# An encoder layer on one Trainium2 core: small vectors loaded into the tile of ones, adaLN's products in four column groups

## The chip, the cores and the metric

The kernel runs on one core of a Trainium2 chip. A core has five engines with queues of their own: PE (TensorE, matrix products; PEld is its loading of weights), DVE (VectorE), ACT (ScalarE), POOL (GpSimd) and SP (SyncE, which here only issues DMAs). Products land in PSUM, everything else on chip lies in SBUF, tiles of 128 partitions. The metric is the device time of one execution in microseconds.

## The reference

One layer (D = 1024, 4 heads of 256) over two sequences with shared weights, a prompt of 1024 tokens and a sample of 256, each with one conditioning vector c. What matters here is the modulation at the head of the layer:

```
mod = c @ w_ada + b_ada                       # (1, 1024) @ (1024, 3072), all fp32
shift, scale, gate = split(mod, 3)
h = rms_norm(x, norm_g) * (1 + scale) + shift
p = h @ w_in                                  # 1024 -> 11280 columns
... short convolution, two-way chunkwise mLSTM, gates ...
out = x + gate * (merged @ w_out);  then rms_norm(out, final_norm_g)
```

Nothing of `p` can be computed before `shift` and `scale` are there, and they take 2048 columns of w_ada, 8 MB, for two vectors.

## The kernel before

**Order of work.** The operations of a stage are recorded first, each with its engine, an estimated cost, what it reads and writes, and a step (a priority). A planner, `Board`, plays them through in a model of its own: per engine a time at which it is free, per DMA an issue cost, a common lane of `KB_US` kilobytes a microsecond and a landing delay. It takes the operation that can start first, or one of a lower step within 0.25 us of it on the same engine, and sends them out in that order; each engine then works through its queue strictly in order. `FIRST` is the time at which SP and the lane are taken to begin. The first stage, up to about 1200 us of the execution, is one such plan, made with `KB_US` 385 and `FIRST` 5.0 (L1283). Buffers of a pool (`misc` for PSUM, `raw`, `wh`, `wl`, `comb`, `acc`) are handed out in the order in which the program names them. So a `misc` buffer named later cannot be taken before adaLN has taken its own, whatever the priorities.

**Setting up (L229 to L270).** POOL writes the identity `ident`, two masks and `ones`, a constant tile of 128 x 128 that later products use for sums over partitions and for spreading a row. A tile `rows` from a pool of its own, on the right side of SBUF, takes the small vectors as rows of 128 (c of both sequences, 2 x 1024 of b_ada, norm_g and others): seven DMAs issued by ACT (L244 to L250). PE turns 80 rows into columns (L253), DVE copies them to `cols` (L254), and the pool of `rows` is closed (L255). Every later tile on the right side may lie where `rows` lay.

**The beginning (L390 to L570).** SP loads w_ada in eight loads `w` 0 to 7 of two 512 KB pieces (a piece is 128 of the 1024 input channels by 512 columns of shift and 512 of scale), the ten blocks of x and the first input weights, in the order `w0, x 0-2, w1, w2, x 3-4, w3, raw (0,8)` and then `raw (0,0), w4 to w7, x 5-7, x 8-9, raw (0,4)`, as far as the tiles are free. Loads 0 to 3 make the first half of the channels of shift and scale (`hf` 0), loads 4 to 7 the second. w_ada and x lie in tiles that later hold the multiplied halves of x: b00, b10, b11 (w_ada; b11H takes w4 and then w7), t2, t3, b11L (x). `early_load` brings weights for the *corners*, twelve small products that are done ahead of the rest.

Of each piece adaLN makes two products (L487). The stationary operand is c, for each piece 128 x 4 with two columns in use (`cz4`, in the spare end of a `big` tile, zeroed by POOL at L465 and filled by DVE at L466); the moving one is 128 x 512 of w_ada. All eight products of one kind sum into `t[0:4, j]`, j = 0 for shift and 1 for scale. After the fourth load of a half the two sums (four partitions each) are copied to SBUF, shift by DVE and scale by ACT (L496), turned by eight small PE transposes into a `misc` buffer (L500), and DVE's `modulation` (L474 to L476) makes s1 and shf of them.

`norm_x` scales the blocks of x on DVE and ACT; `turn_x` transposes them on PE (L449), and ACT (L454) or DVE (L457) applies s1 and shf on the way out of PSUM to `xt`. `both_parts` splits the result into a high and a low part (L381 ACT, L382 DVE), `combine` forms sums and differences (L387 DVE) for a Strassen scheme of seven products. The products with w_in are at L770, all stages' weights being split by ACT (L329) and POOL (L330) out of `raw` tiles, with sums of them by DVE (L642); DVE adds their results (L686).

Of the kernel before, what the change touches and what calls it, by code (L numbers as in the profile page):

```python
# [16 lines left out]
P = 128  # L17
D = 1024
# [22 lines left out]
class Board:  # L41
# [25 lines left out]
    def buf(self, pool, shape, dt, tag, bufs, t=None):  # L67
        b = self.Buf(pool, shape, dt, tag, bufs, t)
        self.places.setdefault((id(pool), tag), []).append(b)
        return b  # L70

    def op(self, eng, us, f, r=(), w=(), after=(), low=False, slack=0.0):

        o = self.Op()
        o.eng, o.us, o.f, o.low, o.step, o.n, o.played, o.slack = eng, us, f, low, self.step, len(self.ops), False, slack
        o.before = set(after)
        for t in r:
            if t in self.writer:
                o.before.add(self.writer[t])
        for t in w:  # L80
            o.before.update(self.readers.get(t, ()))
            if t in self.writer:
                o.before.add(self.writer[t])
        for t in w:
            self.writer[t], self.readers[t] = o, []
        for t in r:
            if t not in w:
                self.readers.setdefault(t, []).append(o)
        o.before.discard(o)
        o.bufs = list(dict.fromkeys(b for t in (*r, *w) for b in (t if isinstance(t, tuple) else (t,)) if isinstance(b, self.Buf)))  # L90
        for b in o.bufs:
            b.users.append(o)
        self.ops.append(o)
        return o
# [87 lines left out]
def encoder_kernel(  # L182
# [50 lines left out]
    G.affine_select(out=masks[:, 1, :], in_=masks[:, 1, :], pattern=[[1, P]], compare_op=ALU.is_ge,  # L233
                    fill=NEG, base=0, channel_multiplier=-1)
    ones = const.tile([P, P], F32, name="ones")
    G.memset(ones[:], 1.0)
    zero = const.tile([P, 1], F32, name="zero")
    V.memset(zero[:], 0.0)


    RC, RNG, RMH, RCW, RCB, RSH, NR = 0, 16, 24, 32, 56, 64, 80
    r0stack = ctx.enter_context(ExitStack())
    rows = r0stack.enter_context(tc.tile_pool(name="rows", bufs=1, side="right")).tile([P, P], F32, name="rows")
    A.dma_start(rows[0:8, :], c_prompt.rearrange("a (r p) -> (a r) p", p=P))  # L244
    A.dma_start(rows[8:16, :], c_sample.rearrange("a (r p) -> (a r) p", p=P))
    A.dma_start(rows[RSH:RSH + 16, :], b_ada[0, 0:2 * D].rearrange("(r p) -> r p", p=P))
# [5 lines left out]
    pt = psA.tile([P, 512], F32, tag="misc", name="misc")  # L252
    PE.transpose(pt[:, :NR], rows[:NR, :], ident[:NR, :NR])  # L253
    V.tensor_copy(cols[:, :NR], pt[:, :NR])  # L254
    r0stack.close()  # L255
    mhq = const.tile([P, KT], F32, name="mhq")
    V.tensor_scalar(out=mhq[:], in0=cols[:, RMH:RMH + 8], scalar1=0.25, scalar2=None, op0=ALU.mult)

# [131 lines left out]
    def beginning():  # L390
        junks = [((lambda b=b: b[:, 0:D]), b) for b in (big(), big())]

        def cz4():
            return junks[0][1][:, D:D + 32].rearrange("p (k s) -> p k s", s=4)

        def load_wa(i):

# [65 lines left out]
        cv_ = cols[:, 0:16].rearrange("p (s k) -> p k s", s=2)  # L463
        ctok = ("c",)
        op("POOL", .15, lambda: G.memset(cz4(), 0.0), w=[junks[0][1], ctok])  # L465
        op("DVE", .15, lambda: V.tensor_copy(cz4()[:, :, 0:2], cv_), r=[ctok], w=[ctok])  # L466
        pada = {}

        def modulation(hf, pm):

            ks = slice(4 * hf, 4 * hf + 4)
            pmc = pm[:, 0:32].rearrange("p (h k l s) -> p h k l s", h=2, l=2, s=2)[:, :, :, 0]
            wide = (lambda c: cols[:, c + 4 * hf:c + 4 * hf + 4].unsqueeze(2).to_broadcast([P, 4, 2]))
            V.tensor_tensor(out=s1[:, ks], in0=pmc[:, 1], in1=wide(RSH + 8), op=ALU.add)  # L474
            V.scalar_tensor_tensor(out=s1[:, ks], in0=s1[:, ks], scalar=1.0, in1=wide(RNG), op0=ALU.add, op1=ALU.mult)
            V.tensor_tensor(out=shf[:, ks], in0=pmc[:, 0], in1=wide(RSH), op=ALU.add)  # L476

        def adaln(i):

            hf = i // 4  # L480
            if i == 0:
                pada.update((n, buf(psX, [P, 2, 512], F32, "acc", 3)) for n in range(2))
            t = pada[hf]
            for n, (wa, tok) in enumerate(wa_at[i]):
                kt = 2 * (i % 4) + n
                for j in range(2):
                    op("PE", .88, lambda j=j, kt=kt, wa=wa: PE.matmul(  # L487
                        t[0:4, j, :], cz4()[:, kt, :], wa()[:, j * 512:(j + 1) * 512],
                        start=kt == 0, stop=kt == KT - 1), r=[ctok, tok], w=[(t, j)])
            if i % 4 < 3:  # L490
                return
            pm = misc_buf()
            for j in range(2):
                m, f = buf(cp, [P, 4, P], F32, "comb", 5), (V.tensor_copy, A.copy)[j]
                row = (lambda m=m: m[0:4].rearrange("p a b -> p (a b)"))
                op(("DVE", "ACT")[j], .6, lambda j=j, f=f, row=row: f(row(), t[0:4, j, :]), r=[(t, j)], w=[m])  # L496

                def turn_mod(j=j, row=row):
                    for r in range(4):
                        PE.transpose(pm[:, 16 * j + 4 * r:16 * j + 4 * r + 4], row()[:, r * P:(r + 1) * P], ident[0:4, 0:4])  # L500

                op("PE", .25, turn_mod, r=[m], w=[(pm, j)])
            op("DVE", .6, lambda: modulation(hf, pm), r=[(pm, 0), (pm, 1)], w=[("s1", hf)])

        def fetch(*items):

# [72 lines left out]
    def misc_buf():  # L579
        return buf(psA, [P, 512], F32, "misc", 2)  # L580
# [698 lines left out]
    for ws in ws_c:  # L1279
        for w in ws:  # L1280
            for b in w:
                b.open = True
    board.KB_US, board.FIRST = 385.0, 5.0  # L1283
    board.play()
    board.KB_US, board.FIRST = Board.KB_US, Board.FIRST
    rstack.close()
# [593 lines left out]
```

## Time and profile before

| | us |
|---|---|
| median of 3 runs | 1692.64 (1692.21 to 1693.99) |
| the profiled execution | 1692.12 |
| its span, first to last instruction | 1690.3 |
| PE busy in it | 1648.8 (98%) |
| DVE / ACT / POOL busy | 989.9 / 575.0 / 677.2 |

A profile page shows one execution: busy times, the span in slices, DMA queues, the chain of waits that ended last, and the costliest groups of instructions. The trace behind it answers narrower questions: who waited for whom, the busy time and the granted clock of TensorE in any stretch, the instructions in order of time. A row of the timeline is start, length, engine, line, operation, the tile written and the tile read, a count, and in brackets how long the engine had been idle and what ended that. `SPq` and `ACTq` are the queues that issue DMAs. A matmul in full fp32 appears as two instructions, one for each pass.

### The profile page before, as it was taken

Reading aid. Unit: us, or ns where it says so; the run is one execution under the profiler, and the core shown is the slowest. Engines: PE = TensorE matmul, PEld = TensorE weight load, DVE = VectorE, ACT = ScalarE, POOL = GpSimd, SP = SyncE. Lnnn points to the kernel's source line nnn. Section 1 sums busy time; section 2 is a strip of 40 time slices with the busy share of each in tenths; the row PEclk is TensorE's granted clock in tenths of the full one; section 3 lists DMA queues with packets and bytes.
Section 4 is the critical chain, followed back from the end, with each engine's and each line's share of the span. In section 5 each row is a group of like instructions: output and inputs, shape, how many; then the busy total and the mean of one; then the engine's idle time right before and its main releaser. Section 6 shows DMA issues by size and latency. Waiting matters only on the chain.

```text
span 1690.3 us, 27664 instructions
## 1 busy us (share of the span) xinstructions
PE 1648.8 (98%) x10526; PEld 1562.4 (92%) x10526; DVE 989.9 (59%) x1688; ACT 575.0 (34%) x1117; POOL 677.2 (40%) x499
## 2 busy tenths in 40 slices
PE   7999999999999999999999999999999999999997
PEld 2699999999999999999999999999988899898985
DVE  4694434556556565566656886662257677555645
ACT  3552332124444222222222212111256665333322
POOL 1133333335565566667666543333210101323412
PEclk9999999999999999999999999999999999999999
DMA  9334325324554222222222556458878855773631
GB/s 318 109 125 139 117 88 125 76 71 128 152 144 111 59 69 69 82 70 67 59 74 74 136 138 145 121 128 269 268 241 293 275 170 177 245 249 105 244 103 63
DMA packets 281527, 240.81 MB, mean 142 GB/s; under 512 B 96068, under 2 KB 236596, under 8 KB 281396
## 3 DMA queue, kind: packets, MB, share of 16 engines
q1 hardware_dynamic: 281216, 239.01, 46.5%
q8 instruction: 83, 1.36, 0.3%
q14 instruction: 48, 0.39, 0.1%
q10 hardware_dynamic: 180, 0.04, 0.0%
HBM read 170.12 MB, written 68.89 MB: 141 GB/s over the span
## 4 chain that ended last, share of the span: by engine, by line
PE 89%; DMA 4%; DVE 4%; SPq 1%; ACT 1%; issue 1%; ACTq 0%; DVEq 0%
PE acc L770 62%; PE u L1399 3%; PE qc L1359 2%; PE accd L1554 2%; PE accd L1555 2%; PE accd L1556 2%; PE accd L1767 2%; PE accd L1768 2%; PE accd L1766 2%; PE acc L1622 2%; PE acc L1621 2%; PE acc L1623 2%; DMA raw<-in_w_in_dram 1%; SPq L318 1%; PE misc L1482 1%; DVE xt L387 1%
## 5 line engine op out<-in xcount | busy, mean ns | idle before, releaser
L330 POOL TENSOR_TENSOR wl<-comb,wh 128x512 fp32r<-128x512 f32 x176 | 246.4, 1400 | 288.0 <-ACT wh L329 268.5
L686 DVE TENSOR_TENSOR q<-acc,q 128x640 f32<-128x640 f32 x272 | 220.8, 819 | 220.3 <-PE acc L770 218.2
L330 POOL TENSOR_TENSOR wl<-raw,wh 128x512 fp32r<-128x512 f32 x136 | 190.6, 1402 | 236.3 <-ACT wh L329 224.4
L770 PE MATMUL acc<-xt,wh 128*128 128x320 f32 x1408 | 265.0, 310 | 2.2 <-DVE xt L382 2.2
L770 PEld LDWEIGHTS acc<-xt,wh 128*128 128x128 f32 x1408 | 220.9, 188 | 3.5 <-DVE xt L382 3.2
L329 ACT CAST wh<-comb 128x512 fp32r<-128x512 f32 x176 | 109.0, 619 | 298.6 <-PE acc L770 288.6
L329 ACT CAST wh<-raw 128x512 fp32r<-128x512 f32 x136 | 84.4, 620 | 269.3 <-PE acc L770 207.3
L770 PE MATMUL acc<-xt,wl 128*128 128x320 f32 x704 | 160.4, 309 | 0.0
L1582 POOL TENSOR_TENSOR wl<-raw,wh 128x512 fp32r<-128x512 f32 x28 | 36.6, 1310 | 224.9 <-ACT wh L1581 175.9
L770 PEld LDWEIGHTS acc<-xt,wl 128*128 128x128 f32 x704 | 117.7, 188 | 0.0
L642 DVE TENSOR_TENSOR comb<-raw 128x512 f32<-128x512 f32 x88 | 72.5, 824 | 43.3 <-DMA raw<-in_w_in_dram 18.4
L837 POOL TENSOR_TENSOR big<-big,q 128x640 f32<-128x640 f32 x48 | 78.2, 1630 | 35.6 <-DVE q L686 27.2
L586 ACT ACTIVATE q<-q,zero 128x640 f32<-128x640 f32 x76 | 63.1, 831 | 79.7 <-DVE q L686 75.3
L642 DVE TENSOR_TENSOR comb<-raw,comb 128x512 f32<-128x512 f32 x44 | 46.1, 1047 | 62.6 <-POOL wl L330 62.5
L770 PE MATMUL acc<-b00H,wh 128*128 128x320 f32 x352 | 81.6, 312 | 0.0
L770 PE MATMUL acc<-b10H,wh 128*128 128x320 f32 x352 | 80.2, 308 | 0.8 <-ACT q L700 0.8
L1554 PE MATMUL accd<-y,wh 128*128 128x320 f32 x256 | 80.3, 314 | 0.6 <-DVE og L1532 0.6
L770 PE MATMUL acc<-b11H,wh 128*128 128x320 f32 x352 | 80.7, 310 | 0.0
L770 PE MATMUL acc<-t2H,wh 128*128 128x320 f32 x352 | 80.4, 309 | 0.0
L770 PE MATMUL acc<-t3H,wh 128*128 128x320 f32 x352 | 80.3, 309 | 0.0
L770 PE MATMUL acc<-t3L,wh 128*128 128x320 f32 x352 | 80.2, 309 | 0.0
L770 PE MATMUL acc<-t3H,wl 128*128 128x320 f32 x352 | 80.2, 309 | 0.0
(312 smaller groups left out, 4120.8 us busy)
## 6 DMA issues: line engine op xcount, KB each, us to landing
raw<-in_w_in_dram SPq DMA_DIRECT2D x108, 256.0 KB
raw<-in_w_in_dram SPq DMA_DIRECT2D x40, 512.0 KB
th<-th_dr SPq DMA_DIRECT2D x32, 320.0 KB
th_dr<-q SPq DMA_DIRECT2D x28, 320.0 KB
raw<-in_w_proj_conv_dram SPq DMA_DIRECT2D x16, 512.0 KB
raw<-in_w_proj_mlstm_dram SPq DMA_DIRECT2D x16, 512.0 KB
raw<-in_w_out_dram SPq DMA_DIRECT2D x16, 512.0 KB
k<-kn_dr SPq DMA_DIRECT2D x56, 128.0 KB
```

Source lines behind the costliest of these rows:

```text
L329: op("ACT", .63, lambda: A.copy(wh[:], src()), r=r, w=[wh])
L330: op("POOL", 1.4, lambda: G.tensor_tensor(out=wl[:], in0=src(), in1=fp(wh[:]), op=ALU.subtract), r=[*r, wh], w=[wl])
L586: A.activation(out, in_, AF.Tanh, bias=zero[:, 0:1], scale=0.5)
L642: op("DVE", .9, lambda: V.tensor_tensor(out=t[:], in0=x(), in1=y(), op=o), r=[x.tok, y.tok], w=[t])
L686: op("DVE", .82, lambda: V.tensor_tensor(out=two(dst()), in0=acc[:, :, 0:TQ], in1=two(t()), op=ALU.add), r=[acc, t.tok], w=[dst.tok])
L770: PE.matmul(acc[:, q, 0:TQ], st_[:, k_, :], m_[:, q * TQ:(q + 1) * TQ], start=k_ == 0 and n == 0, stop=k_ == 3 and n == 2)
L837: op("POOL", 1.65, lambda: G.tensor_tensor(out=dst(), in0=dst(), in1=t(), op=ALU.mult), r=[dst.tok, t.tok], w=[dst.tok])
L1359: PE.matmul(pq[:, 0:HD + 2], qTs[i][:, kd, c * P:(c + 1) * P], C[:, kd, :], start=kd == 0, stop=kd == 1)
L1399: PE.matmul(pu[:, db, 0:HD + 2], k[:, db * P:(db + 1) * P], wv[:], start=True, stop=True)
L1554: PE.matmul(accs[q][:, :TQ], wh, yH, start=kt == 0, stop=False)
L1555: PE.matmul(accs[q][:, :TQ], wh, yL, start=False, stop=False)
L1582: op("POOL", 1.36, lambda wh=wh, wl=wl, src=src: G.tensor_tensor(out=wl[:], in0=src(), in1=fp(wh[:]), op=ALU.subtract), r=[raw, wh], w=[wl])
```

## The change

Four things are changed.

`rows` is no longer a tile of its own: the small vectors are loaded into `ones`, and POOL writes the ones there later, behind the zeroing of c. The pool of `rows` and its closing go.

c's stationary operand becomes 128 x 32 (two columns in use). Each product takes one of four groups of 32 columns of the array, `tile_position=(0, g)`, with g = 32 * (2n + j): n the piece of the load, j shift or scale. The sums land in four groups of 32 partitions of one PSUM bank, each over four of the eight pieces. Two products of a piece are one operation of the plan at 1.1 instead of two at 0.88.

After the fourth load one DVE copy takes all 128 partitions. Four products with `sel`, a 128 x 4 choice of columns made from the identity, turn the sums, add the two groups that belong together and drop the empty columns, instead of eight transposes. ACT's copy goes.

`FIRST` is 1.0 instead of 5.0 for this first plan.

```
     ones = const.tile([P, P], F32, name="ones")
-    G.memset(ones[:], 1.0)
...
-    r0stack = ctx.enter_context(ExitStack())
-    rows = r0stack.enter_context(tc.tile_pool(name="rows", bufs=1, side="right")).tile([P, P], F32, name="rows")
+    rows = ones
...
-    r0stack.close()
...
-            return junks[0][1][:, D:D + 32].rearrange("p (k s) -> p k s", s=4)
+            return junks[0][1][:, D:D + 256].rearrange("p (k s) -> p k s", s=32)
...
         op("POOL", .15, lambda: G.memset(cz4(), 0.0), w=[junks[0][1], ctok])
+        op("POOL", .2, lambda: G.memset(ones[:], 1.0), r=[ctok], w=["ones"])
         op("DVE", .15, lambda: V.tensor_copy(cz4()[:, :, 0:2], cv_), r=[ctok], w=[ctok])
         pada = {}
+        sel = const.tile([P, 2, 2], F32, name="sel")
+        half = (lambda i: ident[:, 64 * i:64 * i + 64].rearrange("p (j r) -> p j r", r=32)[:, :, 0:2])
+        op("DVE", .15, lambda: V.tensor_tensor(out=sel[:], in0=half(0), in1=half(1), op=ALU.add), w=["sel"])
...
-            pmc = pm[:, 0:32].rearrange("p (h k l s) -> p h k l s", h=2, l=2, s=2)[:, :, :, 0]
+            pmc = pm[:, 0:16].rearrange("p (k h s) -> p h k s", h=2, s=2)
...
-                for j in range(2):
-                    op("PE", .88, lambda j=j, kt=kt, wa=wa: PE.matmul(
-                        t[0:4, j, :], cz4()[:, kt, :], wa()[:, j * 512:(j + 1) * 512],
-                        start=kt == 0, stop=kt == KT - 1), r=[ctok, tok], w=[(t, j)])
+                def mm(n=n, kt=kt, wa=wa):
+                    for j in range(2):
+                        g = 32 * (2 * n + j)
+                        PE.matmul(t[g:g + 32, 0, :], cz4()[:, kt, :], wa()[:, j * 512:(j + 1) * 512],
+                                  start=i % 4 == 0, stop=i % 4 == 3, tile_position=(0, g))
+                op("PE", 1.1, mm, r=[ctok, tok], w=[t])
...
-            pm = misc_buf()
-            for j in range(2):
-                m, f = buf(cp, [P, 4, P], F32, "comb", 5), (V.tensor_copy, A.copy)[j]
-                row = (lambda m=m: m[0:4].rearrange("p a b -> p (a b)"))
-                op(("DVE", "ACT")[j], .6, lambda j=j, f=f, row=row: f(row(), t[0:4, j, :]), r=[(t, j)], w=[m])
-                def turn_mod(j=j, row=row):
-                    for r in range(4):
-                        PE.transpose(pm[:, 16 * j + 4 * r:16 * j + 4 * r + 4], row()[:, r * P:(r + 1) * P], ident[0:4, 0:4])
-                op("PE", .25, turn_mod, r=[m], w=[(pm, j)])
-            op("DVE", .6, lambda: modulation(hf, pm), r=[(pm, 0), (pm, 1)], w=[("s1", hf)])
+            pm, m = misc_buf(), buf(cp, [P, 4, P], F32, "comb", 5)
+            op("DVE", .65, lambda: V.tensor_copy(m[:].rearrange("p a b -> p (a b)"), t[:, 0, :]), r=[t], w=[m])
+            def turn_mod():
+                for r in range(4):
+                    PE.matmul(pm[:, 4 * r:4 * r + 4], m[:, r, :], sel[:].rearrange("p j s -> p (j s)"), start=True, stop=True)
+            op("PE", .9, turn_mod, r=[m, "sel"], w=[pm])
+            op("DVE", .6, lambda: modulation(hf, pm), r=[pm], w=[("s1", hf)])
...
-    board.KB_US, board.FIRST = 385.0, 5.0
+    board.KB_US, board.FIRST = 385.0, 1.0
```

## The prediction

> **What bounds the kernel now.** I read the page first, then the waits of SP's queue at the start, the chain of work in order of time, and the busy time by stage.
>
> ```profile
> span 1690.3 us, 27664 instructions
> ```
>
> The page's chain that ended last consists mostly of PE work, so what counts is when PE first runs without gaps and how much it then has left. The page hides what lies before that: who holds back the first load. The waits of SP's queue in the first 20 us show it (time in total, times, longest):
>
> ```profile
> SPq L318 <- DMA rows<-in_norm_g_dram: 2.8, 1, 2.8
> SPq L1867 <- PEq L1867: 0.7, 1, 0.7
> SPq L318 <- DMA rows<-in_conv_w_dram: 0.5, 1, 0.5
> SPq L318 <- PE misc L253: 0.5, 1, 0.5
> SPq L318 <- DMA rows<-in_mh_norm_g_dram: 0.3, 1, 0.3
> SPq L318 <- DMA rows<-in_conv_b_dram: 0.2, 1, 0.2
> ```
>
> SP, which issues every large load, is ready at 0.7 us and then waits 2.8 + 0.5 + 0.5 + 0.3 + 0.2 = 4.3 us for the loads and the turning of `rows`. It has no use for `rows`: the pool of `rows` is closed, and the first tile that SP fills, b00H, lies on the same side of the memory and takes its place. The chain in order of time joins that wait to the rest (start, length, what):
>
> ```profile
> 3.05 1.48 DMA rows<-in_conv_b_dram
> 4.66 0.38 PE misc L253
> 5.06 0.43 SPq L318
> ...
> 45.95 6.63 DMA b11H<-in_w_ada_dram
> ...
> 52.63 1.88 PE acc L487 x4
> ...
> 64.62 0.88 PE acc L770 x6
> ```
>
> From 5.06 us the chain runs through loads to the last piece of w_ada, landed at 45.95 + 6.63 = 52.58 us, then through adaLN's last products. Three stretches of all engines, and one of DVE alone (start:end, length, busy with counts, granted clock, DMA share, GB/s), say what each is bound by:
>
> ```profile
> 5.06:52.58 47.52, 37.73 (x112) 10.82 (x112) 22.98 (x58) 16.39 (x30) 5.94 (x4) 0.96 1.00 343
> 55.64:119.94 64.30, 60.64 (x419) 58.89 (x418) 58.51 (x71) 40.98 (x64) 21.95 (x15) 1.00 0.31 99
> 119.94:1200.00 1080.06, 1075.59 (x7300) 1065.42 (x7300) 612.89 (x794) 305.20 (x521) 546.26 (x394) 1.00 0.40 112
> 53.69:119.30 65.61, 58.54 (x72) 1.00 0.31 97
> ```
>
> First DMA: a share of 1.00 for 47.5 us, with PE idle for 9.8 of them. Then, until 119 us, PE (60.64 of 64.30) and DVE (58.54 of 65.61) are both nearly full, and DVE prepares what PE will multiply. Then PE alone, idle for 1080.06 - 1075.59 = 4.5 us in 1080.
>
> **Part 1: `rows` in the tile of ones.** The constant tile is never given back, so b00H has no predecessor, and SP starts at about 0.7 us. Gain on the path: 4.3 us, if the loads that follow keep their places. They stand one behind the other at a full DMA share, so the last lands at 52.58 - 4.3 = 48.3. The small loads of ACT's queue now travel beside the large ones. Their delay isn't shown, since nothing ran beside them. Bound: none, or all that SP issued before the last of them. SP issues a 512 KB load in about 0.43 us (the 5.06 row), so some six by 3.4 us; 3.1 MB at 343 GB/s is 9 us, which would bring `cols` at 13 us. The lower end is nearer, as the two queues are separate; even the upper end costs little, because adaLN's first half waits for its fourth load anyway (the 25.28 row: 21.0 after the shift), and DVE and POOL stand free:
>
> ```profile
> 25.28 0.08 PEld L487 LDWEIGHTS acc<-b10L,big 128*4 128x4 f32 x1 [0.44 <-DMA b10L<-in_w_ada_dram]
> 2.09 0.12 POOL L465 MEMSET big<- 128x32 f32 x1
> 0.87 0.32 POOL L229 MEMSET masks<- 128x256 f32 x1
> 13.28 1.23 DVE L414 CUSTOM_DVE_ANT_0 big<-t3H 128x1024 f32<-128x1024 f32 x1 [7.60 <-DMA t3H<-in_x_prompt_dram]
> 26.87 5.94 POOL L330 TENSOR_TENSOR wl<-raw,wh 128x512 fp32r<-128x512 f32 x4 [24.66 <-ACT wh L329]
> ```
>
> The zeroing of c grows to the 128x256 form (0.12 to 0.32 us). The ones are now written behind the turning of `rows`; POOL waits there, and behind it stands only the splitting at 26.87, after 24.66 idle us. The sum that makes `sel` is one small DVE operation in the 7.60 idle us before 13.28. All this I count as nothing; without that cover it would be 0.2 us each. `ones` itself is read only by the recurrences and what follows them.
>
> **Part 2: the plan's start, FIRST from 5 to 1.** It issues nothing; it moves the planned arrivals 4 us earlier, as the real ones move, and with the lower PE costs may exchange neighbours. One exchange lies on the path:
>
> ```profile
> 36.06 1.02 PE L487 MATMUL acc<-b11H,big 128*4 128x512 f32 x2
> 38.93 1.07 SPq L318 DMA_DIRECT2D b11H<-in_w_ada_dram  x1
> 40.10 5.76 SPq L318 DMA_DIRECT2D raw<-in_w_in_dram  x2
> 45.95 0.89 SPq L318 DMA_DIRECT2D b11H<-in_w_ada_dram  x1
> raw<-in_w_in_dram SPq DMA_DIRECT2D x108, 256.0 KB
> ```
>
> The last w_ada load overwrites the fifth one's tile, whose products end at 37.1; a pair of `raw` loads slipped between its halves. If those products end earlier in the plan, the second half goes ahead of the pair: 2 x 256 KB at 343 GB/s are 1.5 us. Between 0 and 1.5 I take a gain of 0.7, since the plan's readiness of the two is close.
>
> **Part 3: products in four groups of 32 columns.** Each load of w_ada gives eight matmul instructions (four products, two passes each):
>
> ```profile
> 8.88 5.57 PE L487 MATMUL acc<-b00H,big 128*4 128x512 f32 x8 [3.85 <-DMA b00H<-in_w_ada_dram]
> 15.91 3.60 PE L487 MATMUL acc<-b00L,big 128*4 128x512 f32 x8 [1.46 <-DMA b00L<-in_w_ada_dram]
> ```
>
> At full clock eight end 3.60 us after the first starts, 0.43 us apart: 8 x 8 x 0.43 = 27.5 us over the eight loads. Four products wholly side by side would take 2 x 0.43 = 0.9 us a load; none side by side, 3.4. If instructions start in order, a product's second pass must wait for its first on the same columns, and only the next product's first pass can run beside it: five steps of 0.43, 2.15 us a load. I take that: 8 x 1.3 = 10 us of PE time freed (bounds 0 and 20). Nearly all lies in the stretch where PE waits for loads anyway, so only the end of it counts. The Trainium skill ("TensorE: Matmul & The Clock Gate", Part 3) has matmuls in different column strips run at once, some 4 ns apart; by it a load would take 0.9 us. The same skill ("TensorEngine Tiling (Array Packing)", Key Properties) speaks against the change: changing the tiling mode drains the array, which the transposes in between would pay for. No row here shows either.
>
> The end, after the last arrival (the products' 1.88 us stands above):
>
> ```profile
> 53.69 0.68 DVE L496 COPY comb<-acc 4x512 f32<-4x512 f32 x1 [6.25 <-PE acc L487]
> 54.55 0.57 ACT L496 COPY comb<-acc 4x512 f32<-4x512 f32 x1 [7.97 <-PE acc L487]
> 55.74 0.17 DVE L474 TENSOR_TENSOR s<-misc,cols 128x8 f32<-128x8 f32 x1 [1.38 <-PE misc L500]
> L449 PEld LDWEIGHTS misc<-ident,t3H x16: 137/141/145, 27.8 to 68.2; 128*128 128x128 f32 x16
> ```
>
> Before: products, ACT's copy and its turning: 52.63 to 55.74, 3.1 us. After: two products in three steps of 0.43 (1.3; bounds 0.9 and 1.9), one DVE copy of 0.68 (as long for 128 partitions as for 4, since 512 elements lie in each), four products with 128x128 weights. Weights take 0.14 us; one load each would make 0.6, two passes each 1.1; I take 0.9. With three handovers of 0.1, 3.2 us: no change (bounds -0.7 and +0.9).
>
> **What the freed PE time is worth.** Corner products that need only the first half of s1 can move ahead of the last arrival, out of the stretch where turnings and L770 alternate (the 0.88 us row at 64.62). But until 119 us DVE has 65.61 - 58.54 = 7.1 idle us: no faster PE gains more there, and the idle time mostly follows x's own order. I take 0.5 (bounds 0 and 7.1). After 119.94 the shift passes on, because PE has no slack; a new order could take back some of the 4.5 idle us or add as many: 0.
>
> **Sum:** 4.3 + 0.7 + 0 + 0.5 = 5.5 us. The profiled execution took 1692.12 us (1.8 beyond its span), so 1686.6; the median of the runs is 0.5 higher, 1687.1. A measurement of this kernel can tell about 0.2% from no change, 3.4 us.
>
> **Rivals.** *More (0.12):* products wholly side by side free 20 us, corner work fills the gaps before the last arrival, and the alternating stretch shrinks by DVE's slack. 4.3 + 1.5 + some 5 give 1682, with all 7.1 of it 1680. For it: four weight splits are ready by 33 us. Against it: DVE's 58.5 us have to be done after the arrival.
>
> *A cold PE (0.14):* the granted clock by the microsecond shows that PE, nearly idle, falls to half:
>
> ```profile
> 28.00:29.00 1.00, 0.31 (x3) 0.07 (x1) 0.01 (x1) 1.00 (x3) 1.00 (x1) 1.00 1.04 361
> 30.00:31.00 1.00, 0.78 (x1) 0.09 (x2) 0.47 (x2) 0.43 (x1) 1.00 (x2) 0.50 1.08 406
> 33.00:34.00 1.00, 1.00 (x3) 0.06 (x2) 1.00 (x2) 0.63 (x1) 0.00 (x0) 0.82 1.02 406
> ```
>
> Low load from 28 us, 0.50 from 30, full again after some 3.5 us of work. Shorter products leave longer gaps. If PE is cold when the last piece lands, the end costs 1.3 + 0.9 more, and the next 3.5 us of turnings half as much work, 1.7: 3.9 of the 5.5 go, and 1691 results. Against it: corner products lie ready in those gaps. The Trainium skill ("TensorE: Matmul & The Clock Gate", Part 1) says the same: half rate after an idle window of about 3.4 us; the trace agrees with 0.50 at 30 us.
>
> *Slower (0.08):* the groups don't run side by side and, being seen as little work, never bring the clock up. The first load above ran so: 5.57 us, mostly at double spacing. At twice 0.43 a step, a load's eight instructions take 6.9 us, eight loads 55 us from 8.88 - 4.3 = 4.6 us on: to 59.6 us, past the 54.5 (52.63 + 1.88) at which they end now. Of PE's other work there (37.73 - 27.5, 10 us, some of it time lost cold) I put 4 ahead of the end; then PE, not DMA, sets s1 at about 64 instead of 56: +8, 1700. It decides once a load takes more than 47.5 / 8 = 5.9 us. Against it: the second load ran at full clock with the same duty.
>
> *The wait stays (0.08):* some other owner of b00H's place holds SP back; only parts 2 and 3 act: 1691.4.
>
> **How the numbers follow.** The forecast has 0.58, its own range 1684 to 1689. The range 1681 to 1692.5 takes in the cold PE and the wait that stays, and leaves out half of "more" and the slower case with some chance spread past its ends. Faster than 1689.2: 0.58 + 0.12 and a little of the cold case, 0.72. Within 0.2%: the rest of that and most of the wait that stays, 0.18. Slower: 0.08 and the tail of a worse order later, 0.10.
>
> **What would show it.** Right: SP's first load at about 0.7 us with no wait for `rows`; the last w_ada landing near 47.5 us, with or without the `raw` pair ahead of it; eight L487 instructions in about 2.2 us; PE's last waits for DVE ending near 114 us instead of 119.9; some 4.5 idle us of PE from there to 1200. Wrong: a landing after 50 us, a clock of 0.50 at it, or new idle time in the long stretch of more than 3 us.

## The result and the profile after

The changed kernel takes 1686.66 us (median of 6 runs, 1683.48 to 1689.26), the kernel before on the same chip 1692.51 (1691.66 to 1694.70): a ratio of 0.996, 95% interval 0.9948 to 0.9973. The prediction was 1687.1 in a range of 1681 to 1692.5. The profiled execution took 1686.94 us, 5.18 less than the one of before. The head of its page:

```profile
span 1685.1 us, 27656 instructions
```

The waits of SP's queue in the first 20 us (time in total, times, longest):

```profile
SPq L315 <- DMA b00H<-in_w_ada_dram: 3.1, 1, 3.1
SPq L315 <- DMA b00L<-in_w_ada_dram: 2.7, 2, 1.8
SPq L315 <- DMA ones<-in_b_ada_dram: 1.3, 1, 1.3
```

and the timeline of the same queue, its first loads and, further on, the last w_ada load with its neighbours:

```profile
0.74 0.95 SPq L315 DMA_DIRECT2D b00H<-in_w_ada_dram  x2
4.80 1.99 SPq L315 DMA_DIRECT2D t3H<-in_x_prompt_dram  x2
...
37.39 3.12 SPq L315 DMA_DIRECT2D b11H<-in_w_ada_dram  x2
40.61 3.38 SPq L315 DMA_DIRECT2D raw<-in_w_in_dram  x2
```

The wait for the turning of `rows` is gone and the first load starts at 0.74 instead of 5.06 us. But the load behind it starts only at 4.80: a wait of 3.1 us for the first load itself has come in its place. SP now also waits 1.3 us for a small load, that of b_ada, whose tile it doesn't touch. At the far end the two halves of the last w_ada load now stand together (x2) and the raw pair behind them; before, the pair stood between them.

TensorE's side, adaLN's products, its turning, and the first product of the b22 job (all x is split by then; before at 120.07). The products of the last load's first half, before:

```profile
49.62 1.88 PE L487 MATMUL acc<-b11H,big 128*4 128x512 f32 x4 [0.97 <-DMA b11H<-in_w_ada_dram]
```

and after (PEld is the loading of weights):

```profile
8.47 0.20 PEld L491 LDWEIGHTS acc<-b00H,big 128*32 128x32 f32 x8 [0.91 <-DVE big L464]
8.47 1.94 PE L491 MATMUL acc<-b00H,big 128*32 128x512 f32 x8 [0.70 <-DVE big L464]
...
40.21 1.80 PE L491 MATMUL acc<-b10H,big 128*32 128x512 f32 x8
40.95 0.14 PEld L491 LDWEIGHTS acc<-b10H,big 128*32 128x32 f32 x4 [0.60 <-DMA b10H<-in_w_ada_dram]
...
47.21 1.05 PE L491 MATMUL acc<-b11H,big 128*32 128x512 f32 x4
48.62 1.05 PE L491 MATMUL acc<-b11H,big 128*32 128x512 f32 x4 [0.35 <-DMA b11H<-in_w_ada_dram]
...
50.59 0.95 PE L502 MATMUL misc<-sel,comb 128*128 128x4 f32 x8
...
105.38 0.63 PE L772 MATMUL acc<-xt,wh 128*128 128x320 f32 x2 [3.54 <-DVE xt L379]
...
113.77 0.45 PE L772 MATMUL acc<-b11H,wh 128*128 128x320 f32 x2
```

Two products (four instructions) take 1.05 us instead of 1.88, eight instructions 1.80 instead of 3.60. In the 1.80 the second pair of products waits for its piece of w_ada until 40.95, so that row doesn't show how many can run at once. The row at 8.47 does: there both pieces have landed, all eight weights are loaded within 0.20 us, and eight instructions of 1.06 us each end 1.94 us after the first starts. The four products run wholly side by side, at about half the rate of the later rows, as the first instructions of before did (5.57 us for eight, at 8.88). DVE applies the scale (s1) in this row:

```profile
51.57 0.17 DVE L475 TENSOR_TENSOR s<-misc,cols 128x8 f32<-128x8 f32 x1 [1.16 <-PE misc L502]
```

And the stretches (start:end, length, busy PE, PEld, DVE, ACT, POOL with counts, granted clock, DMA share, GB/s): from s1 to the b22 job, from there to 1200, and two short ones behind TensorE's wait of 3.54 us:

```profile
51.57:113.77 62.20, 58.66 (x403) 57.92 (x403) 55.09 (x71) 40.63 (x63) 20.36 (x14) 0.97 0.29 94
113.77:1200.00 1086.23, 1080.07 (x7315) 1069.44 (x7314) 616.65 (x794) 305.31 (x523) 548.21 (x395) 1.00 0.41 113
106.00:108.00 2.00, 2.00 (x10) 2.00 (x9) 2.00 (x4) 0.81 (x2) 0.00 (x0) 0.50 0.00 0
108.00:110.00 2.00, 2.00 (x12) 2.00 (x12) 1.83 (x3) 0.00 (x0) 0.00 (x0) 0.72 0.00 0
```

The same five points in both kernels add up to the whole difference. The products of the last w_ada load start as its halves land, so the first row shows the stream ahead of the raw pair and the second adds the exchange:

| | before | changed | difference |
|---|---|---|---|
| products of the last w_ada load's first half start | 49.62 | 47.21 | -2.41 |
| products of its second half start | 52.63 | 48.62 | -4.01 (-1.60 more) |
| s1 | 55.74 | 51.57 | -4.17 (-0.16 more) |
| b22 job starts | 120.07 | 113.77 | -6.30 (-2.13 more) |
| end of the span | 1690.3 | 1685.1 | -5.2 (+1.1: given back) |

So the early load is worth 2.4 us and not 4.3, the exchange of the raw pair 1.6 and not 0.7, and 2.1 us come out of the stretch behind s1, in which DVE's busy time fell from 58.64 (between the same two points of before) to 55.09. Single profiles settle such terms only roughly: in changed_again below, the same kernel, they are -1.49, -1.65, -0.16 and -1.38, and the rest gains 1.1 more.

### The profile page after: what moved, and what is told of

It is laid out like the page before. It is cut to its first block, busy times and chain, and to the rows that moved or that the text cites. A ratio compares the mean times of both kernels' runs of the same rounds, so it can differ in the third digit from the quotient of the medians.

```text
span 1685.1 us, 27656 instructions
## 1 busy us (share of the span) xinstructions
PE 1639.5 (97%) x10526; PEld 1565.8 (93%) x10526; DVE 993.3 (59%) x1689; ACT 572.8 (34%) x1115; POOL 679.0 (40%) x499
## 3 DMA queue, kind: packets, MB, share of 16 engines
q8 instruction: 83, 1.36, 0.3%
## 4 chain that ended last, share of the span: by engine, by line
PE 66%; DVE 1%; ACT 0%; issue 0%; DMA 0%; POOL 0%; SPq 0%; DVEq 0%; ACTq 0%; POOLq 0%
PE acc L772 38%; PE u L1401 3%; PE qc L1361 3%; PE accd L1556 2%; PE accd L1557 2%; PE accd L1558 2%; PE acc L1623 2%; PE acc L1624 2%; PE acc L1625 2%; PE accd L1770 2%; PE accd L1768 2%; PE accd L1769 2%; PE misc L1484 1%; PE misc L1444 1%; PE misc L1531 1%
## 5 line engine op out<-in xcount | busy, mean ns | idle before, releaser
L1556 PE MATMUL accd<-y,wh 128*128 128x320 f32 x256 | 80.5, 315 | 0.6 <-DVE og L1534 0.6
L1557 PE MATMUL accd<-y,wh 128*128 128x320 f32 x256 | 80.4, 314 | 0.0
L772 PE MATMUL acc<-b00L,wh 128*128 128x320 f32 x352 | 80.2, 309 | 0.1
```

Of the source, the lines that this page charges most:

```text
L772: PE.matmul(acc[:, q, 0:TQ], st_[:, k_, :], m_[:, q * TQ:(q + 1) * TQ], start=k_ == 0 and n == 0, stop=k_ == 3 and n == 2)
L1556: PE.matmul(accs[q][:, :TQ], wh, yH, start=kt == 0, stop=False)
L1557: PE.matmul(accs[q][:, :TQ], wh, yL, start=False, stop=False)
```

## The experiments

The theory: the reordering by the plan, and DVE's time behind s1, carry most of the gain, while a new wait eats much of what the early start should give. Rival: the earlier start and the faster products are the gain by themselves. All ratios are to the kernel before, run on the same chip (its medians were 1692.78, 1693.27 and 1693.05 in the three sets of runs). The first four rows ran together, then changed_again, rows_pool_queue, combine_pool and pool_queue_combine, then the other four. changed_again is the changed kernel once more; s1 and the stretches are of one profile each.

| kernel | median (range, runs) | ratio, 95% interval | s1 | s1 to b22 | DVE busy in it |
|---|---|---|---|---|---|
| rows_alone | 1690.23 (1689.62-1692.13, 11) | 0.9987, 0.9979-0.9996 | 53.83 | 64.30 | 58.87 |
| rows_first | 1690.96 (1687.21-1691.96, 11) | 0.9984, 0.9975-0.9993 | 53.20 | 64.30 | 58.74 |
| rows_first_raw_behind | 1688.95 (1687.33-1690.88, 9) | 0.9977, 0.9968-0.9987 | 51.80 | 64.49 | 58.63 |
| groups_alone | 1687.97 (1686.03-1689.20, 6) | 0.9971, 0.9959-0.9982 | 54.07 | 60.85 | 54.39 |
| changed_again | 1685.25 (1683.06-1686.36, 5) | 0.9953, 0.9939-0.9966 | 52.44 | 62.95 | 55.10 |
| rows_pool_queue | 1686.34 (1683.43-1687.63, 5) | 0.9959, 0.9946-0.9971 | 49.77 | 63.44 | 56.29 |
| combine_pool | 1689.66 (1688.91-1691.83, 11) | 0.9979, 0.9971-0.9988 | 51.20 | 66.30 | 60.74 |
| pool_queue_combine | 1687.32 (1686.00-1689.74, 7) | 0.9970, 0.9960-0.9981 | 49.94 | 66.26 | 60.84 |
| groups_old_plan | 1689.69 (1686.87-1691.83, 11) | 0.9982, 0.9974-0.9991 | 55.11 | 64.08 | 55.91 |
| splits_before_combine | 1686.47 (1686.08-1687.26, 5) | 0.9964, 0.9951-0.9978 | 51.11 | 62.50 | 55.12 |
| kept_warm | 1685.01 (1682.04-1685.85, 5) | 0.9949, 0.9936-0.9961 | 51.44 | 60.89 | 54.39 |
| pool_queue_splits_first | 1682.01 (1680.77-1682.08, 5) | 0.9934, 0.9922-0.9947 | 49.76 | 60.83 | 54.65 |

For changed_again I had expected 1686.7, a spread of some 5 us, and, if the spread came from how fast TensorE runs behind its long wait, a granted clock that goes with the time. The spread was 3.3 us. In the first six runs of the changed kernel the two fastest have the highest clock (0.994 and 0.993 against 0.991), but in changed_again the fastest has 0.992 like the slowest. So where the spread comes from stays open.

**The small vectors alone.** Only the first part of the change, `rows = ones` and the late ones:

```
-    G.memset(ones[:], 1.0)
-    r0stack = ctx.enter_context(ExitStack())
-    rows = r0stack.enter_context(tc.tile_pool(name="rows", bufs=1, side="right")).tile([P, P], F32, name="rows")
+    rows = ones
-    r0stack.close()
+        op("POOL", .2, lambda: G.memset(ones[:], 1.0), r=[ctok], w=["ones"])
```

> The kernel before with part 1 alone: rows in the tile of ones, products as before, FIRST 5. Theory (eight semaphores): the DMAs of SP and ACT share eight completion semaphores, dealt out in turn, and a DMA waits until the one eight places before it has landed; so SP issues two pieces of w_ada at 0.7 us and its third load waits for the first piece until about 4.8. The stream gains the two pieces' share, some 1.5 us, and the raw pair still lies between the halves of the last w_ada load: its last products start at 51.1 instead of 52.6, time 1691. Rival (the start is worth its full length): last products at 48.3, time 1688.

s1 moves by 1.91 us (55.74 to 53.83) and the stretch behind it not at all (64.30 against 64.33). SP's third load starts at 4.34 us, so the wait is here too. The gain of 4.3 us is missed; the new wait belongs to this part.

**The same with the plan's start.** `FIRST` 1.0 instead of 5.0 besides:

```
-    board.KB_US, board.FIRST = 385.0, 5.0
+    board.KB_US, board.FIRST = 385.0, 1.0
```

> Parts 1 and 2: rows in the tile of ones and FIRST 1, products as before. Theory: the plan's start changes no order that counts, so this is as with part 1 alone: raw pair between the halves of the last w_ada load, last products at 51.1, time 1691. Rival (FIRST brings the exchange of the raw pair): last products near 48.7, time 1687 to 1688.

s1 at 53.20, the time not to be told from rows_alone. The raw pair stays where it was, so the new start time of the plan is not what exchanges it.

**What the new wait is.** The seven loads of the small vectors go to GpSimd's queue; everything else is the changed kernel:

```
-    A.dma_start(rows[0:8, :], c_prompt.rearrange("a (r p) -> (a r) p", p=P))
+    G.dma_start(rows[0:8, :], c_prompt.rearrange("a (r p) -> (a r) p", p=P))
...
```

> The changed kernel with the seven loads of rows issued by POOL instead of ACT; they take other semaphores. Theory (eight semaphores): SP's third load follows at 1.7 us without a wait, the whole stream moves another 2.7 to 3 us, last products near 45.8 instead of 48.6, time 2 to 3 us less: 1684. Rival (the wait at 1.7 us is the transfers' own slow start): SP still stops until about 4.8, no change. If POOL's loads come late, cols comes at 8 to 12 us, which costs nothing.

In the compiled program SP's and ACT's DMAs share eight completion semaphores (counters that a landing raises), given out in turn, and a DMA first waits for the one eight places earlier to land. The changed kernel's trace shows it: its record of each DMA names the semaphore that the DMA raises and the one it waits for. Two pieces of w_ada and seven small loads come before SP's next load. This one has the semaphore of the first piece, number 102, and waits for it, although it writes another tile; the piece lands at 4.78 and the load starts at 4.80. Without the seven in that round, the timeline of SP's queue shows no gap:

```profile
0.75 0.94 SPq L315 DMA_DIRECT2D b00H<-in_w_ada_dram  x2
1.74 0.93 SPq L315 DMA_DIRECT2D t3H<-in_x_prompt_dram  x2
...
34.68 3.56 SPq L315 DMA_DIRECT2D b11H<-in_w_ada_dram  x2
```

The last w_ada load is now issued 38.93 - 34.68 = 4.25 us earlier than before: the 4.3 of the prediction. Its first half lands 4.20 us earlier too (45.38 against 49.58 in the records); in the nine profiles with the seven loads on ACT's queue and the early start, that is 1.5 to 2.9. So both the records and the edit show that the wait is the semaphores'. The last products start at 46.81, where 45.8 was expected. The small loads pay for it, being turned at 10.83 instead of 7.40 us: adaLN's first products start at 11.90 instead of 8.47, which isn't on the path. But the median doesn't move against changed_again (1686.34 to 1685.25, intervals overlapping): s1 comes 2.67 us earlier than there, the b22 job only 2.18 (113.21 to 115.39), and 0.56 us earlier than the changed kernel's first profile. TensorE waits for DVE instead:

```profile
104.96 0.90 PE L772 MATMUL acc<-xt,wh 128*128 128x320 f32 x2 [4.92 <-DVE xt L379]
```

**The exchange alone.** rows_first with the raw pair (1, 0) made to read the tokens of the last w_ada load, so that SP's order is the changed kernel's, with the old products:

```
-            load(256, lambda i=i: raw[:, :, i * P:(i + 1) * P], win[:, 4 * j:4 * j + 4, c:c + P], (), [(raw, i)])
+            load(256, lambda i=i: raw[:, :, i * P:(i + 1) * P], win[:, 4 * j:4 * j + 4, c:c + P], [x[1] for x in wa_at[7]] if (j, n) == (1, 0) else (), [(raw, i)])
```

> As parts 1 and 2, and one pair of raw loads is made to follow both halves of the last w_ada load; nothing else is moved, and the products stay 4 columns wide, one after the other. Theory (the order of the loads is what part 3 brings; its faster products bring little): last products start near 49 us, s1 near 52, time within 1.5 us of the changed kernel, 1687 to 1688. Rival (the groups' speed is what counts): no better than parts 1 and 2 alone, 1690 to 1691.

SP's queue in rows_first, the pair between the halves (adaLN's products of the two halves start at 47.11 and 50.09):

```profile
37.18 0.99 SPq L315 DMA_DIRECT2D b11H<-in_w_ada_dram  x1
38.26 5.07 SPq L315 DMA_DIRECT2D raw<-in_w_in_dram  x2
43.42 0.88 SPq L315 DMA_DIRECT2D b11H<-in_w_ada_dram  x1
```

and in rows_first_raw_behind, with adaLN's last products and the first weights of the second half:

```profile
36.43 3.45 SPq L315 DMA_DIRECT2D b11H<-in_w_ada_dram  x2
39.97 3.81 SPq L315 DMA_DIRECT2D raw<-in_w_in_dram  x2
...
46.97 3.60 PE L485 MATMUL acc<-b11H,big 128*4 128x512 f32 x8 [0.92 <-DMA b11H<-in_w_ada_dram]
48.36 0.08 PEld L485 LDWEIGHTS acc<-b11H,big 128*4 128x4 f32 x1 [0.44 <-DMA b11H<-in_w_ada_dram]
```

The first half lands at 46.9, the second just before 48.36: 1.4 us apart instead of 3.0. The exchange is worth the difference, 1.6 us, about the 1.5 that the pair's bytes take. By the trace's records of landings it is the same in all fourteen profiles: 2.97 to 3.04 us between the two landings in the four kernels with the pair between the halves, 1.36 to 1.43 in the ten without. How long issuing the pair holds SP (5.07 us) doesn't show in it. With the old products both halves' work, 3.60 us, lies behind the first half's landing, so s1 gains 1.40 (53.20 to 51.80). It was expected within 1.5 us of the changed kernel and is 2.3 to 3.7 us above: s1 is the changed kernel's, but the stretch behind it is still 64.49 long. So the order of the loads explains s1, and something else shortens the stretch.

**The groups alone, and the groups with the old cost.** First the third part of the change without the others (`FIRST` 5.0, `rows` in its own pool):

> Part 3 alone: products in four column groups, rows in a pool of their own, FIRST 5, SP starts at 5.06 us. Theory: SP's plan puts the last w_ada load ahead of the raw pair, its last products start near 50.2 us instead of 52.6, and DVE's stretch after it is some 2 us shorter as in the changed kernel: 1688 to 1689. Rival (the early start carries the gain): 1692, no change.

s1 gains 1.67, the pair has been exchanged, and the stretch shrinks to 60.85. Then the changed kernel with one number put back, which is only the plan's:

```
-                op("PE", 1.1, mm, r=[ctok, tok], w=[t])
+                op("PE", 1.8, mm, r=[ctok, tok], w=[t])
```

> The changed kernel with one number put back: the plan's cost of a group of two adaLN products is again 1.8 instead of 1.1; the products themselves are issued as in the changed kernel. Theory A (the change's second half works through the order that the plan makes, not through the speed of the products): the raw pair comes back between the two halves of w_ada's last load, the last adaLN products start at 50 to 52 us instead of 48.62 and 49.49, the scale step 3 us behind them, the products of 32 columns still take about 1.05 us for two, the next stretch's splits by VectorE sum to more than 21 us instead of 19.9, and the median is 1688 to 1690.5. Theory B (the speed of the groups itself is the gain): the order matters little and the median is within 1 us of the changed kernel's 1685.3 to 1686.7.

The raw pair is back between the halves, in SP's queue:

```profile
36.43 0.98 SPq L315 DMA_DIRECT2D b11H<-in_w_ada_dram  x1
37.50 4.69 SPq L315 DMA_DIRECT2D raw<-in_w_in_dram  x2
42.28 0.88 SPq L315 DMA_DIRECT2D b11H<-in_w_ada_dram  x1
```

and the granted clock (the number ahead of the DMA share) is down when the last piece lands, as one of the prediction's rivals had it:

```profile
44.00:48.00 4.00, 1.28 (x4) 0.19 (x4) 0.83 (x1) 0.04 (x1) 0.00 (x0) 0.70 1.04 319
48.00:52.00 4.00, 2.88 (x7) 0.58 (x6) 0.28 (x1) 0.00 (x0) 0.00 (x0) 0.50 0.04 15
52.00:56.00 4.00, 4.00 (x19) 4.00 (x19) 0.82 (x4) 0.15 (x1) 0.00 (x0) 0.50 0.00 0
```

TensorE has 1.28 us of work in 44 to 48, falls to half, and s1 comes 5.35 us behind the last products' start (49.76 to 55.11) instead of 2.95. Two products take 1.92 us at that clock:

```profile
46.72 1.92 PE L491 MATMUL acc<-b11H,big 128*32 128x512 f32 x4 [2.85 <-DMA b11H<-in_w_ada_dram]
```

The groups are all there, and without the order that their lower cost brings they are worth nothing in the median: 3.0 and 4.4 us above the two measurements of the changed kernel, and at the ratio of rows_first (0.9982 and 0.9984). The profile is of the slowest of the eleven runs (1691.83), so its low clock and its s1 need not be those of the others. This is theory A, except that I had expected s1 3 us behind the products, and that VectorE's splits summed to 20.6 us and not to over 21. That is most of the way from 23.3 (before, and rows_first) to the changed kernel's 19.9: the shorter splits come with part 3, but they do not hang on that one cost, and which of part 3's other changes to the plan brings them wasn't tried. TensorE, busy 63.15 of 64.08 us, bounds this stretch instead.

**Why the stretch behind s1 is shorter.** The groups of VectorE's splits (busy, mean ns) sum to 8.5 + 4.6 + 3.7 + 3.5 + 3.0 = 23.3 us before and 6.3 + 4.1 + 3.3 + 3.1 + 3.1 = 19.9 us after, 24 operations of one shape in both. The first and the third of the five, before:

```profile
L382 DVE TENSOR_TENSOR xt<-xt 128x640 fp32r<-128x640 f32 x8 | 8.5, 1094 | 0.3
L382 DVE TENSOR_TENSOR b10L<-xt,b10H 128x640 fp32r<-128x640 f32 x4 | 3.7, 922 | 0.3 <-ACT b10H L381 0.3
```

and after:

```profile
L379 DVE TENSOR_TENSOR xt<-xt 128x640 fp32r<-128x640 f32 x8 | 6.3, 816 | 0.3
L379 DVE TENSOR_TENSOR b10L<-xt,b10H 128x640 fp32r<-128x640 f32 x4 | 3.3, 823 | 1.2 <-ACT b10H L378 1.2
```

What stretches a split is in the timeline of before, DVE and POOL side by side:

```profile
109.97 3.39 DVE L382 TENSOR_TENSOR xt<-xt 128x640 fp32r<-128x640 f32 x3
110.70 1.92 DVE L382 TENSOR_TENSOR xt<-xt 128x640 fp32r<-128x640 f32 x1
...
110.34 1.60 POOL L330 TENSOR_TENSOR wl<-comb,wh 128x512 fp32r<-128x512 f32 x1 [1.72 <-ACT wh L329]
```

and of after, where POOL does nothing from 103.91 to 116.25:

```profile
104.52 3.02 DVE L379 TENSOR_TENSOR xt<-xt 128x640 fp32r<-128x640 f32 x4
```

Three splits take 3.39 us beside one split of POOL, four take 3.02 without. Of the three, one takes 1.92, the one at 110.70 that starts while POOL is busy, and the others 0.81. By the Trainium skill ("SBUF — State Buffer", "SBUF: two separate sides") a VectorE operation with two SBUF inputs and a GpSimd operation that reads SBUF exclude each other, and whichever starts second waits for the other's end. The trace agrees: the long one starts 0.36 us after POOL's split and ends 0.68 us after that split's end at 111.94, close to the 0.75 to 0.81 that a VectorE split takes alone. To try it, the four subtractions of one `combine` were moved from VectorE to GpSimd, 4.08 us of work:

```
-                combine(B21, B21, B22)
+                combine(B21, B21, B22, ALU.subtract, "POOL", 1.65, G)
```

> The changed kernel with the last four differences (b21 minus b22, for t4) on POOL instead of DVE. Theory (DVE sets the end of the stretch to 114 us, and PE stands idle and then runs at half clock for it): DVE loses some 4 us of work there, PE's wait of 3.5 us for the split of xt shrinks to under 1, the b22 products start near 111 instead of 113.8, time 2 to 3 us less. Rival (the wait is the plan's order, not DVE's load): no change, or the slower POOL delays t4 and it is 1 to 2 us longer.

The gain is missed, and the kernel is slower than changed_again on the same chip. VectorE's splits sum to 28.2 us instead of 19.9, and those of t2L, beside GpSimd's subtractions, take twice as long:

```profile
L379 DVE TENSOR_TENSOR t2L<-xt,t2H 128x640 fp32r<-128x640 f32 x4 | 6.7, 1712 | 0.0
L379 DVE TENSOR_TENSOR t3L<-xt,t3H 128x640 fp32r<-128x640 f32 x4 | 5.2, 1364 | 0.0
...
L379 DVE TENSOR_TENSOR b10L<-xt,b10H 128x640 fp32r<-128x640 f32 x4 | 3.3, 822 | 1.2 <-ACT b10H L378 1.2
```

Taking 4.08 us of work from VectorE cost it 8.3 in its other work. So the collision is shown, and with it that VectorE's time in this stretch depends on when POOL works. Together with the loads on GpSimd's queue the result is the same (t2L 1712 ns again), and the early start doesn't make up for it:

> Both of the last two. If the two act on different stretches their gains add: 4 to 6 us less than the changed kernel, 1681 to 1683. If DVE's load hides the earlier stream, no better than the better of the two.

**The order on VectorE and the clock behind a wait.** In the changed kernel the subtractions of that `combine` stand ahead of t1's splits, for which TensorE waits 3.54 us, and then runs at a granted 0.50. Three kernels take this apart. The splits ahead of the `combine` (the plan's text only, the same operations):

```
-                combine(B21, B21, B22)
                 both_parts("t1")
+                combine(B21, B21, B22)
```

> The changed kernel with VectorE's splits of t1 put ahead of combine(B21, B21, B22), whose four operations take 4.08 us; nothing else is moved. Theory A (TensorE's wait of 3.54 us at 101.7 us is only VectorE's order): that wait falls below 1 us, TensorE's clock does not fall to half behind it, the first product of the b22 job comes 1 to 3 us earlier and the median is 1 to 3 us below the changed kernel's. Theory B (the stretch between the scale step and the b22 job is bound by VectorE's sum of 55.1 us): the wait comes back in front of t4's or b22's products, the b22 job starts within 1 us of 113.8, and the median is the same within 1 us; if POOL's split now runs beside t1's, those take 1.9 us instead of 0.81 each and the median is 1 to 3 us higher.

The wait before t1 shrinks to 1.34 us and another one comes up before t4, and the clock falls behind that one (0.50 from 110 to 112):

```profile
103.60 0.56 PE L772 MATMUL acc<-xt,wh 128*128 128x320 f32 x2 [1.34 <-DVE xt L379]
...
108.74 0.66 PE L772 MATMUL acc<-xt,wh 128*128 128x320 f32 x2 [2.24 <-DVE xt L379]
```

The b22 job starts at 113.61: theory B. Next, the order as it was, and 20 products that nothing reads put into the wait:

```
+                if warm and k_ == 0 and n == 1:
+                    for x in range(20):
+                        PE.matmul(warm[:, 0:TQ], wh[:, 0, :], mh[:, 0:TQ], start=True, stop=True)
```

> The changed kernel with 20 products more, of 128x320 into a spare buffer that nothing reads, in the middle of the t1 job where TensorE waits for VectorE; the work is added, nothing that the kernel computes is changed. Theory A (the half clock behind TensorE's wait costs 1.1 to 2.1 us): the granted clock stays above 0.9 from 104 to 110 us, the t1 and t4 jobs behind the wait take about 7.1 us instead of 8.39, the b22 job starts 1 to 2 us earlier and the median is 1 to 2 us lower. Theory B (VectorE's splits set the pace there at either clock, or the added products themselves cost what they save): the b22 job and the median stay within 0.7 us.

```profile
101.56 3.10 PE L775 MATMUL misc<-xt,wh 128*128 128x320 f32 x20
105.18 0.57 PE L777 MATMUL acc<-xt,wh 128*128 128x320 f32 x2 [0.52 <-DVE xt L379]
...
112.33 0.46 PE L777 MATMUL acc<-b11H,wh 128*128 128x320 f32 x2
```

The clock stays at 1.00, and from the end of the wait to the b22 job it is 112.33 - 105.18 = 7.15 us instead of 113.77 - 105.38 = 8.39 (and 9.24 in changed_again): 1.2 to 2.1 us for a cold restart. groups_alone, whose clock stayed at 1.00 behind its wait without any added work, needs the same 114.92 - 107.77 = 7.15. In the median, 1685.01, the gain can't be told from changed_again. Last, both earlier edits together, the small loads on GpSimd's queue and the splits first:

> The changed kernel with both: the seven small loads of rows on GpSimd's queue, so that SyncE's third load does not wait for a place among the completion semaphores, and t1's splits ahead of combine(B21, B21, B22). Theory A (the early stream, 1.7 us with these loads, was lost to VectorE's order in the next stretch): the last adaLN products start near 46.8 us, the b22 job before 112 us, and the median is 1682 to 1684.5. Theory B (the stretch is bound by VectorE's sum, whatever the order): the b22 job starts at 112.5 to 114 us and the median is 1685 to 1687, as with the loads' queue alone.

```profile
107.10 0.57 PE L772 MATMUL acc<-xt,wh 128*128 128x320 f32 x2 [2.39 <-DVE xt L379]
...
110.59 0.46 PE L772 MATMUL acc<-b11H,wh 128*128 128x320 f32 x2
```

The last products start at 46.80, the b22 job at 110.59, and the median is 1682.01, as theory A had it, and the lowest here. Its five runs (up to 1682.08) all lie below the five of splits_before_combine on the same chip (from 1686.08). Neither edit alone gave anything that could be told from the changed kernel, and even this one's ratio overlaps that of changed_again (0.9922 to 0.9947, 0.9939 to 0.9966). TensorE waited 2.39 us here and kept its full clock, where splits_before_combine waited 2.24 and lost it. The b22 job starts 2.62 us earlier than in rows_pool_queue, of which 1.2 to 2.1 can be the clock, so what the order of the splits gives by itself is not shown. The length of a single wait doesn't decide the clock: behind 2.76 us in combine_pool it stayed at 1.00, behind 2.77 in pool_queue_combine it fell to 0.50.

The column of the stretch agrees: the three profiles at full clock with VectorE busy for 54.4 to 54.7 us take 60.83, 60.85 and 60.89; the four where the clock fell, VectorE at 55.1 to 56.3, take 62.20 to 63.44; and those with VectorE at 58.6 to 58.9 take 64.3 to 64.5 at full clock.

## Why the prediction came out right, and which steps of it were wrong

The time was right, by 0.4 us at the medians, but that it came so close was luck. In the profile the five terms were off by -1.9, +0.9, +0.2, +1.6 and -1.1 us, which cancel to -0.3.

- **Part 1, 4.3 us "if the loads that follow keep their places".** They kept their order and not their distance: 2.4 us came at the last load, and 1.5 to 2.9 in nine profiles. I had asked what the small loads would suffer from the large ones, and not what the large ones would suffer from the small: with seven small loads in the round of eight places, the third large one comes to the place of a large one that is still under way. One wait took the place of the other, which was no rival of mine (I had the old wait staying, not a new one coming). rows_pool_queue shows the full 4.25.
- **Part 2, the exchange, 0.7 of at most 1.5.** It happened whole, and was worth 1.6 us, about the pair's bytes: the bound was right, and the 0.7 was only a choice between yes and no. But it wasn't the plan's start that brought it but the products' lower cost (rows_first without, groups_alone with the exchange).
- **Part 3, eight instructions in 2.15 us, the end unchanged.** Five steps of 0.43 was wrong: I let a product's second pass hold up the next products, but where the data is there the eight instructions start four at a time (8.47 and, by the trace's records, 9.33), in two steps. That is my lower bound, 0.9 at the full rate as an estimate from 0.43 a step. No whole load of the changed kernel's profile ran so at the full rate, as the pieces land one by one. The drain that spoke against the change doesn't show either: at 40.21 the groups start while the transpose before them (40.00, 0.27 us) is still ending. At the end two products took two steps, 1.05, and the gain was 0.16, inside the bounds. By itself the speed is worth nothing in the median (groups_old_plan).
- **The freed PE time, 0.5 with bounds 0 and 7.1.** The stretch gave 2.13, and would have given 3.5 at full clock. The step that failed is "no faster PE gains more there": it took VectorE's 58.5 us as a fixed amount of work. In the new order fewer splits met POOL's work, and VectorE needed 3.5 us less.
- **Later, 0.** TensorE's idle time from the b22 job to 1200 is 1086.23 - 1080.07 = 6.2 us instead of 4.5, and 1.1 us of the span were given back. changed_again's span from there on is 1569.1, 1.1 below before's 1570.2, and over all fourteen profiles it lies between 1568.1 and 1572.7, so this term is not settled by single profiles.
- **The rivals.** The cold TensorE did not come when the last piece landed (1.00 from 44 to 52), but half a stretch later, and in groups_old_plan just where I had put it. "More", 1682, had the products wholly side by side, which came true, and names the right place of the gain, the alternating stretch. But the gain there is 2.1 and not 5 or more, and it comes with less work for VectorE (3.5 us, mostly splits that no longer meet POOL's), which I had taken as fixed.

Of what should have shown it, the first load at 0.74 us without a wait for `rows` came true. TensorE's last long wait for VectorE ends at 105.38 already, but the b22 job behind those waits starts at 113.77, near the 114 I gave and by another sum. The landing near 47.5 came at 48.6.

## What to carry to other kernels

When a wait is removed from the head of a queue, look for what the next instruction waits for: semaphores and ring places that several queues share count as resources too, and many small transfers between two large ones use them up. The estimated costs that a planner is given can be worth more than the speed of the instructions, and can be tried by themselves with one number. Before calling a stage bound by an engine's busy time, look whether the same operation has two durations in it: that part of the busy time is a collision, and an order can remove it.

## What was unexpected of the hardware

- A VectorE operation on two SBUF operands of 128x640 takes 0.75 to 0.82 us alone, 1.92 when it starts just behind one of GpSimd's, and 1.71 on average over the four of t2L beside GpSimd's subtractions and splits; moving work from VectorE to GpSimd made VectorE slower (28.2 against 19.9 us for the same 24 operations).
- Full fp32 products in different groups of 32 columns run beside each other: four whose data had landed take 1.94 us where groups_old_plan needs 1.92 for two at half clock, and two at the full clock 1.05 instead of 1.88. What looks like half speed in the row of 1.80 is the wait for data.
- The granted clock fell to 0.50 behind waits of 2.24, 2.77, 3.45, 3.54 and 4.92 us, and stayed at 1.00 behind waits of 2.39, 2.76 and 3.42 us. The Trainium skill ("TensorE: Matmul & The Clock Gate", "What's actually happening") has a window of about 3.4 us that runs freely, so that the point of the change depends on where the work falls in it; the waits of 2.24 and 2.39, and of 2.76 and 2.77 us, with different outcomes agree with that, though no run here moved the window itself. A wait of 2.24 us is shorter than such a window, so the clock fell here without one that was wholly idle.
